# Weight tiles of two row blocks instead of one in a two-layer encoder step on one Trainium2 core

## The chip, the cores and the metric

The kernel runs on one core of one Trainium2 chip. The metric is the time of one execution on the device, in microseconds (us); a comparison takes the median of several runs. TensorE is called PE below, its weight loads PEld, VectorE DVE, ScalarE ACT, GpSimd POOL and SyncE SP, as in the profile.

## What is computed

One step of an encoder with two layers, for 384 tokens: two blocks of 128 from a prompt, and one block that holds 16 tokens of each of eight running streams. All data are 32-bit floats. Cut to what matters here:

```python
# layer 0: one projection, then two kinds of attention side by side
p  = rmsnorm(x, norm0_g) @ w_in0        # 2048 x 8200: fox q,k,v,z, stick-breaking q,k,v,z, forget logits
fo = softmax(q k^T * scale + F_q - F_k) @ v           # F: running sums of log forget gates
so = a @ v                # a: stick-breaking weights from log_sigmoid(z) and reversed running sums
h  = x + concat(fo * silu(z), so * silu(z)) @ w_out0                     # 2048 x 2048
# layer 1: spatial gating in chunks of 128 positions
u, v, z = split(rmsnorm(h, norm1_g) @ w_in1)                             # 2048 x 12288
h  = h + (u * (W_s @ layernorm(v) + b) * silu(z)) @ w_out1               # 4096 x 2048
y  = rmsnorm(h, final_g)
```

The new keys, values, forget gates and the normalised v rows are outputs too.

## The kernel before

**How a product is formed.** A weight matrix is read in blocks of 128 rows by 512 columns. TensorE multiplies in a shortened 32-bit form (`fp32r`), so each operand is split into a high and a low part, and a product is the sum of three: high by high, high by low, low by high. A block goes through four steps. SP loads it into a tile `raw` (256 KB; L72-75, L218-220, L121). ScalarE copies it, shortened, into `whi` (L84). VectorE subtracts that from `raw` into `wlo` (L86). TensorE multiplies it with each of the three token blocks (L100 high by high, L101 by the low part of the weights, L102 by the low part of the activations): 9 matmuls. Activations are split the same way by `split` (L89-91), so L90 and L91 stand for these, and for all other splits.

**The rings.** `raw` has five buffers of 128x512 (L73), `whi` and `wlo` four each (pool `wp`, L52; a buffer is 576 elements wide, L30). A buffer comes free when its last reader is done: that of `raw` after L86, those of the parts after L102.

**Columns.** `dense_nat` (L107-126) computes 512 output columns for 384 tokens: the rows in pairs of blocks, 18 matmuls a pair, into three banks of PSUM. A pair takes 4.08 us on TensorE (18 times 0.2265, its pitch in the trace). At some pairs `between` calls other work (a hook): attention heads, transposes, splits of activations. That work is put behind the split of the pair before (L116-117).

**The stages, in order of time.**

- The first columns (k of quad 0, L280-324): `first_unit` splits block 0, block 1, then pairs, in turn with the transposes and splits of the activations (L278 is the low part of these); the order on each engine is fixed by `then`.
- `values_first` (L473-498): v of quad 0 in tiles of two row blocks by 256 columns, again 128x512 a tile.
- Four quads of four heads each (L535-657): 0 and 1 with the forgetting attention, 2 and 3 with the stick-breaking one. Each projects k, q, z and v (quad 0 v ahead of q), runs the sigmoid of z by a chain on ScalarE and VectorE (L649-653), and hangs its heads as hooks on the columns of the next (L583-588). The heads (L674-768) use both engines and have their own transfers.
- The residual columns of layer 0 (`w_out0`, L840-869). Their `raw` tiles are taken from the ring and, in turn, from buffers of the heads that are idle by then (`kcache`, `vcache`; `places`, L825-837): of 13 blocks five from the ring.
- Layer 1: two ordinary columns of v; the second has four hooks `token_sums` (L911-936) on it. Then the other columns in pairs by a scheme of seven products instead of eight ("seven", L961-1033). That code has its own tiles, `sraw`, `shi` and `slo`, of 128x1024 (L941-950), loaded by 512 KB, and its own pool.
- Two ordinary columns of z and u, then the output projection `w_out1` in four rounds of `out1` (L1179-1186). Beside these the spatial gating of eight chunks is prepared (L1215-1259): its gate is transposed (L1255) and split (L1257). The last four row blocks are split early into spare buffers by `last_split` (L1319-1323).

**What sets the order.** Within the rules above a scheduler orders the instructions of each engine, with a timing model of its own that runs when the program is built; so the places of instructions move when durations or buffers change, also where the source doesn't.

## Time and profile before

| | |
|---|---|
| median of 3 runs | 1742.53 us (1740.14 to 1742.74) |
| profiled execution | 1743.44 us, span in the profile 1741.7 |
| TensorE busy | 1728.0 us, 99%, granted clock at full speed in all slices |
| VectorE, ScalarE, GpSimd busy | 1290.0 (74%), 828.2 (48%), 363.6 (21%) |
| DMA | 424.41 MB, mean 244 GB/s |
| splits of ordinary tiles | 450 on ScalarE (0.630 us each), 450 on VectorE (0.700) |
| splits of 128x1024 in the seven-product columns | 280 on each (1.061 and 1.220) |

How to read it: the span is divided between work and waits for each engine. A row of a group names the line, the engine, the operation and output <- inputs, then busy time and the mean of one, then idle time just before these instructions with what ended most of it. "PEld d L101 <- DVE wlo L86: 2.1, 7, 0.5" in the table of waits reads: weight loads for L101 waited for the VectorE instruction of L86, 2.1 us in 7 waits, the longest 0.5. A row of the timeline gives start, duration, engine, line, operation, tiles, and in brackets an idle time and what ended it. Since TensorE is busy nearly all the time, its waits are what to look for.

### The profile page before, as it was taken

How to read it: one execution, taken by the hardware profiler on the slowest of the kernel's cores; microseconds unless marked ns; L12 is line 12 of the kernel's file. 1: busy time of each engine (PE TensorE's matmuls, PEld its weight loads, DVE VectorE, ACT ScalarE, POOL GpSimd, SP SyncE). 2: the span in 40 equal slices, each digit the busy share in tenths (PEclk: the TensorE clock that was granted, in tenths of full speed). 3: DMA queues.
4: the chain of work that ended last, by engine and by line, in shares of the span. 5: the costliest groups of instructions: out<-in, count | busy, mean ns of one | idle time of the engine just before them, and what ended most of it. 6: DMA issues, size and time to landing. Idle time of an engine off the chain costs nothing. (4 is left out here: it accounts for less than half of the span.)

```text
span 1741.7 us, 23995 instructions
## 1 busy us (share of the span) xinstructions
PE 1728.0 (99%) x8323; PEld 1426.8 (82%) x8323; DVE 1290.0 (74%) x1794; ACT 828.2 (48%) x1259; POOL 363.6 (21%) x517
## 2 busy tenths in 40 slices
PE   9999999999999999999999999999999999999998
PEld 8988888887887888888878888888888887888887
DVE  6337566448347555589999999999998887787766
ACT  5435344337336344455545555555554543343344
POOL 6425544212312211100200100000000033423200
PEclk9999999999999999999999999999999999999999
DMA  8788989868877877769998989888988679879653
GB/s 233 189 226 187 279 216 223 239 184 206 235 211 186 254 195 163 188 204 333 304 304 298 313 275 320 285 294 272 320 292 271 220 248 339 255 228 305 181 159 114
DMA packets 235498, 424.41 MB, mean 244 GB/s; under 512 B 22552, under 2 KB 66128, under 8 KB 235376
## 3 DMA queue, kind: packets, MB, share of 16 engines
q1 hardware_dynamic: 174992, 312.40, 58.2%
q0 software_dynamic: 29552, 94.34, 20.0%
q10 hardware_dynamic: 30832, 16.13, 3.2%
q8 instruction: 65, 1.06, 0.3%
q14 instruction: 57, 0.47, 0.1%
HBM read 374.48 MB, written 48.29 MB: 243 GB/s over the span
## 5 line engine op out<-in xcount | busy, mean ns | idle before, releaser
L101 PE MATMUL d<-wlo,slot 128*128 128x512 f32 x1389 | 540.5, 390 | 0.2
L102 PE MATMUL d<-whi,slot 128*128 128x512 f32 x1389 | 539.8, 390 | 0.3 <-DVE slot L91 0.3
L86 DVE TENSOR_TENSOR wlo<-raw,whi 128x512 fp32r<-128x512 f32 x450 | 310.4, 700 | 306.4 <-ACT whi L84 305.1
L84 ACT ACTIVATE whi<-raw 128x512 fp32r<-128x512 f32 x450 | 281.5, 630 | 457.2 <-PE d L102 363.4
L100 PE MATMUL d<-whi,slot 128*128 128x512 f32 x1389 | 493.9, 391 | 0.8 <-ACT whi L84 0.6
L90 ACT ACTIVATE shi<-sraw 128x1024 fp32r<-128x1024 f32 x280 | 296.0, 1061 | 265.5 <-DVE sraw L970 115.5
L91 DVE TENSOR_TENSOR slo<-sraw,shi 128x1024 fp32r<-128x1024 f32 x280 | 336.6, 1220 | 25.5 <-ACT shi L90 24.1
L100 PEld LDWEIGHTS d<-whi,slot 128*128 128x128 f32 x1389 | 260.4, 188 | 59.2 <-issue 1.8
L101 PEld LDWEIGHTS d<-wlo,slot 128*128 128x128 f32 x1389 | 260.8, 188 | 55.1 <-DVE wlo L86 2.1
L102 PEld LDWEIGHTS d<-whi,slot 128*128 128x128 f32 x1389 | 260.7, 188 | 54.9 <-DVE slot L91 0.7
L958 PE MATMUL a<-slo,slot 128*128 128x512 f32 x720 | 280.5, 390 | 0.6 <-DVE slo L91 0.6
L957 PE MATMUL a<-shi,slot 128*128 128x512 f32 x720 | 264.8, 391 | 1.4 <-ACT shi L90 1.2
L970 DVE TENSOR_TENSOR sraw<-sraw,sraw 128x1024 f32<-128x1024 f32 x160 | 195.1, 1219 | 4.6 <-DMA sraw<-in_w_in_dram 4.3
L957 PEld LDWEIGHTS a<-shi,slot 128*128 128x128 f32 x720 | 135.0, 188 | 34.2 <-ACT shi L90 5.0
L958 PEld LDWEIGHTS a<-slo,slot 128*128 128x128 f32 x720 | 135.1, 188 | 29.2 <-DVE slo L91 1.5
L959 PE MATMUL a<-shi,slot 128*128 128x512 f32 x400 | 155.7, 389 | 0.0
L959 PE MATMUL a<-shi,suml 128*128 128x512 f32 x320 | 124.5, 389 | 0.0
L959 PEld LDWEIGHTS a<-shi,slot 128*128 128x128 f32 x400 | 75.1, 188 | 15.8
L1054 POOL DMA_DIRECT2D gd<-slot x7 | 3.9, 557 | 346.9 <-DVE slot L898 346.9
L464 POOL DMA_DIRECT2D slot<-d x48 | 44.1, 924 | 136.8 <-DVE wlo L86 54.2
L959 PEld LDWEIGHTS a<-shi,suml 128*128 128x128 f32 x320 | 60.1, 188 | 12.5
L957 PE MATMUL d<-shi,slot 128*128 128x512 f32 x160 | 62.3, 389 | 0.0
(311 smaller groups left out, 1840.0 us busy)
## 6 DMA issues: line engine op xcount, KB each, us to landing
sraw<-in_w_in_dram SPq DMA_DIRECT2D x320, 512.0 KB, 5.2
raw<-in_w_in_dram SPq DMA_DIRECT2D x320, 256.0 KB, 4.1
raw<-in_w_out_dram SPq DMA_DIRECT2D x175, 256.0 KB, 4.5
slot<-d POOLq DMA_DIRECT2D x48, 192.0 KB, 5.4
d<-slot ACTq DMA_DIRECT2D x24, 256.0 KB, 3.9
vd<-slot POOLq DMA_DIRECT2D x8, 768.0 KB, 4.7
gd<-slot POOLq DMA_DIRECT2D x8, 768.0 KB, 6.6
v<-vd POOLq DMA_DIRECT2D x8, 768.0 KB, 8.7
```

The costliest lines, as they stand in the source:

```text
L84: highs.append(S.activation(hi, raw, AF.Copy).ins)
L86: splits.append(V.tensor_tensor(out=lo, in0=raw, in1=f32(hi), op=ALU.subtract).ins)
L90: S.activation(hi_out, src, AF.Copy)
L91: return V.tensor_tensor(out=lo_out, in0=src, in1=f32(hi_out), op=ALU.subtract).ins
L100: PE.matmul(o, lhsT=his[k][:, t], rhs=hi[:, 0, :], start=(k == first), stop=False)
L101: PE.matmul(o, lhsT=his[k][:, t], rhs=lo[:, 0, :], start=False, stop=False)
L102: mm = PE.matmul(o, lhsT=los[k][:, t], rhs=hi[:, 0, :], start=False, stop=(k == last))
L464: r = G.dma_start(blk[32 * j:32 * j + 32].rearrange("p h (a d) -> p (h a) d", d=32), d[:, :, 32 * j:32 * j + 32].rearrange("h (a p) d -> p ...
L957: PE.matmul(o, lhsT=xh, rhs=hi[:, j, :], start=(opens and u + j == 0), stop=False)
L958: PE.matmul(o, lhsT=xh, rhs=lo[:, j, :], start=False, stop=False)
L959: PE.matmul(o, lhsT=xl, rhs=hi[:, j, :], start=False, stop=(ends and u == 3 and j == 1))
L970: return V.tensor_tensor(out=out, in0=x, in1=y, op=op)
```

## The change

All ordinary weight tiles hold two row blocks. A pair of `dense_nat` is one transfer of 512 KB, one copy on ScalarE and one subtraction on VectorE, both 128x1024; TensorE reads each half as before. `raw` has three buffers of 128x1024, `whi` and `wlo` two each, 1088 elements wide; per partition the rings take 29,696 bytes in place of 28,672. `values_first` takes four row blocks of 256 columns a tile in place of two, and its two hooks move from tiles 4 and 7 of 8 to tiles 2 and 3 of 4. In the first columns blocks 0 and 1 are still loaded and split apart, each pair of loads sharing a raw tile, while from block 2 on a pair is split at once. `places` gives whole tiles, three of seven from the ring. `last_split` loads single blocks into halves of a raw tile. The unused `eight` goes. The seven-product columns are not touched.

The instructions: 7711 on PE in both; ACT has 943 in place of 1216, DVE 1446 in place of 1706, SP 617 in place of 862. In the changed kernel the lines of this text have other numbers: L84 is L91, L86 is L93, L90/91 are L97/98, L100/101/102 are L107/108/109, L649/650 are L655/656 (and L651 L657), L731 is L737, L739 is L745, L1140 is L1132, L1184 is L1176, L1255 is L1247.

```diff
-WPITCH = 576
+WPITCH = 1088
...
-    wp = ctx.enter_context(tc.tile_pool(name="wp", bufs=4))
+    wp = ctx.enter_context(tc.tile_pool(name="wp", bufs=2))
...
-    def wload(src, nk, ncols, queue=nc.sync):
-        raw = wp.tile([P, nk, ncols], F32, tag="raw", bufs=5, name=nm("raw"))
-        queue.dma_start(raw, src.rearrange("(k p) c -> p k c", p=P))
+    def wraw(nk=2):
+        return wp.tile([P, nk, 1024 // nk], F32, tag="raw", bufs=3, name=nm("raw"))
+    def whalf(tag):
+        return wp.tile([P, WPITCH], F32R, tag=tag, name=nm(tag))
+    def wload(src, nk=2):
+        raw = wraw(nk)
+        nc.sync.dma_start(raw, src.rearrange("(k p) c -> p k c", p=P))
         return raw
-    def wunit(src, nk, ncols, raw=None, behind=()):
...
+    def halves(tag):
+        return whalf(tag)[:, :1024].rearrange("p (k c) -> p k c", k=2)
+    def wunit(raw, behind=()):
+        hi = halves("whi")
...
+        lo = halves("wlo")
         splits.append(V.tensor_tensor(out=lo, in0=raw, in1=f32(hi), op=ALU.subtract).ins)
-        return hi, lo
+        return [(hi[:, j:j + 1, :], lo[:, j:j + 1, :]) for j in range(2)]
...
-            ws = []
-            for k in (kp, kp + 1):
-                src = w[(k0 + k) * P:(k0 + k + 1) * P, c0:c0 + 512]
-                raw = raws() if raws else None
-                if raw is not None:
-                    nc.sync.dma_start(raw, src.rearrange("(k p) c -> p k c", p=P))
-                ws.append(wunit(src, 1, 512, raw, behind=behind))
+            raw = (raws and raws()) or wraw()
+            nc.sync.dma_start(raw, w[(k0 + kp) * P:(k0 + kp + 2) * P, c0:c0 + 512].rearrange("(k p) c -> p k c", p=P))
+            ws = wunit(raw, behind=behind)
...
         def load_raw():
             k = len(raws)
-            raws.append(wload(w_in0[k * P:(k + 1) * P, 1024:1536], 1, 512))
+            if k % 2 == 0:
+                both.append(wraw())
+            raws.append(both[k // 2][:, k % 2:k % 2 + 1, :])
+            nc.sync.dma_start(raws[k], w_in0[k * P:(k + 1) * P, 1024:1536].rearrange("(k p) c -> p k c", p=P))
...
-                nxt = [first_unit(k) for k in groups[i + 1]]
+                nxt = first_unit(groups[i + 1])
...
-            for u in range(KT // 2):
-                if u in (4, 7) and between:
+            for u in range(KT // 4):
+                if u > 1 and between:
...
-                raw = wload(w_in0[u * 256:(u + 1) * 256, c0:c0 + 256], 2, 256)
+                raw = wload(w_in0[u * 512:(u + 1) * 512, c0:c0 + 256], 4)
...
-                if n % 13 < 5:
+                if n % 7 < 3:
                     yield None
...
+                if not spare:
+                    both = wraw()
+                    spare.extend(both[:, j, :] for j in range(2))
+                raw = spare.pop(0)
+                nc.sync.dma_start(raw, wlast(*ck))
```

**How the order moves.** On TensorE, at the start of a pair in the q columns of quad 0, before (d are the three banks, slot_128 and slot_129 the high and low parts of the activations, whi_1198/wlo_1200 the first block, whi_1204 the second):

```order
L100 MATMUL d_1131<-whi_1198,slot_128 128x512
L100 MATMUL d_1132<-whi_1198,slot_128 128x512
L100 MATMUL d_1133<-whi_1198,slot_128 128x512
L101 MATMUL d_1131<-wlo_1200,slot_128 128x512
L102 MATMUL d_1131<-whi_1198,slot_129 128x512
L100 MATMUL d_1131<-whi_1204,slot_128 128x512
L101 MATMUL d_1132<-wlo_1200,slot_128 128x512
```

And after (one tile whi_1070/wlo_1072 for both blocks):

```order
L107 MATMUL d_1039<-whi_1070,slot_124 128x512
L107 MATMUL d_1040<-whi_1070,slot_124 128x512
L107 MATMUL d_1041<-whi_1070,slot_124 128x512
L108 MATMUL d_1039<-wlo_1072,slot_124 128x512
L109 MATMUL d_1039<-whi_1070,slot_125 128x512
L107 MATMUL d_1039<-whi_1070,slot_124 128x512
L108 MATMUL d_1039<-wlo_1072,slot_124 128x512
```

In both, three high-by-high products stand first. Before, the fourth matmul needs the low part of the first block; after, it needs that of the whole pair.

On ScalarE, where the heads of quad 2 and the sigmoid of its z run (pr, z and l are the heads' tiles, gz and slot_4192 the sigmoid's), before:

```order
L733 ACTIVATE l_4272<-l_4272 128x384
L733 ACTIVATE l_4283<-l_4283 128x288
L649 ACTIVATE slot_4192<-gz_4188 128x512 x3
L650 ACTIVATE slot_4192<-slot_4192 128x512
L84 ACTIVATE whi_4408<-raw_4406 128x512
L650 ACTIVATE slot_4192<-slot_4192 128x512 x2
```

After:

```order
L91 ACTIVATE whi_3866<-raw_3864 128x1024
L655 ACTIVATE slot_3668<-gz_3664 128x512 x3
L745 ACTIVATE pr_3739<-z_3740 128x384
L656 ACTIVATE slot_3668<-slot_3668 128x512 x3
L745 ACTIVATE pr_3739<-z_3751 128x288
L657 ACTIVATE slot_3668<-slot_3668 128x512
L737 ACTIVATE l_3777<-z_3775 128x384
L91 ACTIVATE whi_3890<-raw_3888 128x1024
```

Before, a split stands after four operations of the sigmoid; after, seven of these and three of the heads stand between one split and the next.

On VectorE in the last stage, around the transpose of a gate (gTt) and its low half (slot_13922, in the changed kernel slot_12567), before:

```order
L86 TENSOR_TENSOR wlo_13899<-raw_13895,whi_13897 128x512
L1255 STREAM_TRANSPOSE gTt_13919<-blk_13748 128x1536
L1184 TENSOR_TENSOR slot_13593<-d_13742,slot_13593 128x512
L1184 TENSOR_TENSOR slot_13593<-d_13743,slot_13593 128x512
L1184 TENSOR_TENSOR slot_13593<-d_13744,slot_13593 128x512
L91 TENSOR_TENSOR slot_13922<-gTt_13919,slot_13921 128x1536
L86 TENSOR_TENSOR wlo_13929<-raw_13925,whi_13927 128x512
```

After:

```order
L93 TENSOR_TENSOR wlo_12544<-raw_12540,whi_12542 128x1024
L1247 STREAM_TRANSPOSE gTt_12564<-blk_12309 128x1536
L1176 TENSOR_TENSOR slot_12304<-d_12370,slot_12304 128x512
L1176 TENSOR_TENSOR slot_12304<-d_12371,slot_12304 128x512
L1176 TENSOR_TENSOR slot_12304<-d_12372,slot_12304 128x512
L93 TENSOR_TENSOR wlo_12574<-raw_12570,whi_12572 128x1024
L1132 SCALAR_TENSOR_TENSOR v_12443<-v_12443,mvr,lg_12445 128x512
L98 TENSOR_TENSOR slot_12567<-gTt_12564,slot_12566 128x1536
```

The gate's low half stood ahead of the next split of weights, and now stands behind it.

## The prediction

> **What bounds the kernel now.** I read the profile's page first, then the busy time by windows, then who waits for whom on the weight loads, then the timeline at the places where TensorE waits. The page, engine totals, TensorE's clock and the four groups that split weights into high and low parts:

> ```profile
> PE 1728.0 (99%) x8323; PEld 1426.8 (82%) x8323; DVE 1290.0 (74%) x1794; ACT 828.2 (48%) x1259; POOL 363.6 (21%) x517
> ...
> PEclk9999999999999999999999999999999999999999
> ...
> L86 DVE TENSOR_TENSOR wlo<-raw,whi 128x512 fp32r<-128x512 f32 x450 | 310.4, 700 | 306.4 <-ACT whi L84 305.1
> L84 ACT ACTIVATE whi<-raw 128x512 fp32r<-128x512 f32 x450 | 281.5, 630 | 457.2 <-PE d L102 363.4
> L90 ACT ACTIVATE shi<-sraw 128x1024 fp32r<-128x1024 f32 x280 | 296.0, 1061 | 265.5 <-DVE sraw L970 115.5
> L91 DVE TENSOR_TENSOR slo<-sraw,shi 128x1024 fp32r<-128x1024 f32 x280 | 336.6, 1220 | 25.5 <-ACT shi L90 24.1
> ```

> TensorE is busy for 1728.0 of 1741.7 us at full clock. A busy PE need not be PE at its peak, so I ask whether the width of a weight tile changes its pace. The windows answer that; the third lies in the stretch of seven-product columns, which already uses tiles of 128x1024:

> ```profile
> 410.00:426.00 16.00, 15.90 (x71) 12.83 (x70) 13.80 (x30) 15.29 (x33) 3.39 (x4) 1.00 0.94 213
> 750.00:800.00 50.00, 50.00 (x223) 41.39 (x222) 47.01 (x72) 28.56 (x40) 3.00 (x5) 1.00 0.79 277
> 1250.00:1300.00 50.00, 50.00 (x222) 41.19 (x221) 47.40 (x48) 28.38 (x31) 0.53 (x1) 1.00 0.87 294
> ```

> Columns: window, its length, then busy time and count of PE, PEld, DVE, ACT, POOL, clock, DMA share. 50 us hold 221 to 222 weight loads on ordinary tiles (second row) and on wide ones (third): 0.226 us a matmul in both. The change alters neither the number of matmuls nor their pace. It can change the time only through TensorE's waits. Today these are few:

> ```profile
> PEld a L957 <- ACT shi L90: 5.0, 12, 1.3
> PEld d L101 <- DVE wlo L86: 2.1, 7, 0.5
> PEld d L100 <- ACT whi L84: 1.6, 3, 0.8
> ```

> The last two are all that TensorE waits for ordinary weight tiles: 3.7 us. That is the most that better feeding of these tiles can win. The first belongs to the seven-product columns, whose code isn't touched.

> **The cost of the splits.** Two narrow splits take 2 x 0.630 on ScalarE and 2 x 0.700 on VectorE, a wide one 1.061 and 1.220: 0.20 and 0.18 us less for each two blocks. Neither engine sets the end, so this is worth nothing by itself. What matters is how late a tile may be. A steady place of before, with the reads of the old tile, the split and the first reads of the new one:

> ```profile
> 304.90 0.19 PEld L102 LDWEIGHTS d<-whi,slot 128*128 128x128 f32 x1
> 305.58 0.19 PEld L102 LDWEIGHTS d<-whi,slot 128*128 128x128 f32 x1
> ...
> 309.88 0.64 PEld L100 LDWEIGHTS d<-whi,slot 128*128 128x128 f32 x3
> 310.56 0.19 PEld L101 LDWEIGHTS d<-wlo,slot 128*128 128x128 f32 x1
> ...
> 305.55 1.31 ACT L84 ACTIVATE whi<-raw 128x512 fp32r<-128x512 f32 x2 [4.43 <-PE d L102]
> ...
> 306.21 1.37 DVE L86 TENSOR_TENSOR wlo<-raw,whi 128x512 fp32r<-128x512 f32 x2 [1.87 <-ACT whi L84]
> ```

> The first block's buffer is read last at 304.90, ScalarE starts 0.65 later, the first low part is there at 306.21 + 0.69 = 306.90 and is read at 310.56: 3.7 us to spare. A wide buffer comes free only with its second block, read last at 305.58. So 305.58 + 0.65 = 306.23, the high part ends at 307.29, the low part at 307.29 + 0.03 + 1.22 = 308.54; the new order also reads three high parts first, so it is needed at 310.56: **2.0 us to spare**. The slack falls by 1.7 us everywhere. Where nothing else is late this costs nothing: the tile being read, 18 matmuls or 4.08 us, hides the split. Where ScalarE, VectorE or a load is more than 2.0 us late, TensorE now waits. I go through these places.

> [...]

> *Start.* Blocks 2 and 3 become one tile, in a ring where blocks 0 and 1 take a whole tile each.

> ```profile
> 8.76 1.30 ACT L282 ACTIVATE whi<-raw 128x512 fp32r<-128x512 f32 x2 [0.77 <-DMA raw<-in_w_in_dram]
> ...
> 11.49 0.39 PE L101 MATMUL d<-wlo,slot 128*128 128x512 f32 x1
> 11.72 0.40 PE L102 MATMUL d<-whi,slot 128*128 128x512 f32 x1
> ...
> 10.70 1.14 DVE L278 SCALAR_TENSOR_TENSOR slot<-a,gT,slot 128x384 fp32r<-128x384 f32 x2
> ```

> The wide split starts between 8.76 and 9.4 (its second half waits for its load), so the low part ends between 11.1 and 11.7, and the low part of the activations, 0.57 of VectorE behind it, between 11.7 and 12.3, for reads at 11.49 and 11.72. 0 to 0.6 us late; I take 0.3.

> *First quad, loads late.* Around 100 us ScalarE waits for the loads themselves:

> ```profile
> 97.38 0.63 ACT L84 ACTIVATE whi<-raw 128x512 fp32r<-128x512 f32 x1 [4.76 <-DMA raw<-in_w_in_dram]
> 100.02 0.63 ACT L84 ACTIVATE whi<-raw 128x512 fp32r<-128x512 f32 x1 [2.02 <-DMA raw<-in_w_in_dram]
> 102.50 0.63 ACT L84 ACTIVATE whi<-raw 128x512 fp32r<-128x512 f32 x1 [1.85 <-DMA raw<-in_w_in_dram]
> ...
> 101.31 0.64 PEld L100 LDWEIGHTS d<-whi,slot 128*128 128x128 f32 x3
> ...
> 103.18 0.19 PEld L100 LDWEIGHTS d<-whi,slot 128*128 128x128 f32 x1 [0.78 <-ACT whi L84]
> ```

> Today TensorE works on the block of 100.02 from 101.31 while that of 102.50 lands, and waits 0.9 in all. As one tile nothing of them can start before 102.50: high part at 103.56, 2.25 after 101.31; low part at 104.81, another 0.57 over. That is 2.8, or +1.9 on today's. Against it, three raw tiles hold six blocks where five buffers held five, so a load can be issued one block (9 matmuls, 2.0 us) earlier; if all of that arrives, the wait goes (-0.9). The middle is +0.5; I take +1.0, because the loads here are paced by their landing, about 2.5 us a block, and not by their issue.

> *Stick-breaking quads, ScalarE late.* In the window 410 to 426 above ScalarE is busy 15.29 of 16 us, and a low part is late there, and again at the next quad:

> ```profile
> 412.87 1.66 ACT L649 ACTIVATE slot<-gz 128x512 f32<-128x512 f32 x3
> ...
> 421.45 0.19 PEld L101 LDWEIGHTS d<-wlo,slot 128*128 128x128 f32 x1 [0.52 <-DVE wlo L86]
> ...
> 559.75 0.19 PEld L101 LDWEIGHTS d<-wlo,slot 128*128 128x128 f32 x1 [0.49 <-DVE wlo L86]
> ```

> The split was 3.7 + 0.5 = 4.2 late. Four pairs of splits save 0.8 of that; past the new slack of 2.0 it waits 1.4, 0.9 more than now. By the new order the longest stretch between two splits has seven operations of 128x512 (0.55 each, the first row) and three small ones (about 0.4): 5.1 + 1.06 against 4.08 is 2.1 late, at the edge of the slack, which would end today's 0.5. Between -0.5 and +0.9 each; the chain between ScalarE and VectorE that made today's wait is not in that count, so I take +0.45 each, +0.9.

> *Residual columns of the first layer.* A load lands late:

> ```profile
> 703.88 0.63 ACT L84 ACTIVATE whi<-raw 128x512 fp32r<-128x512 f32 x1 [7.04 <-DMA raw<-in_w_out_dram]
> 704.70 1.87 ACT L84 ACTIVATE whi<-raw 128x512 fp32r<-128x512 f32 x3 [0.18 <-DMA raw<-in_w_out_dram]
> ...
> 704.57 0.53 PEld L100 LDWEIGHTS d<-whi,slot 128*128 128x128 f32 x3 [0.66 <-ACT whi L84]
> ```

> Now 0.6 is lost. A wide split could start at 704.70: high part at 705.76, 1.8 after TensorE was ready at 703.95, low part 0.6 more: 2.4, or +1.8; one block earlier, -0.6. I take +0.7. *Token sums* (second window): VectorE is busy 47.01 of 50 us; the splits give back 12 x 0.18 = 2.2 us of that, the lost slack takes 1.7 from each tile: 0 to +1.0, I take +0.3.

> *Last stage.* Transposed blocks of the gate hold up both splitting engines:

> ```profile
> 1528.72 1.49 ACT L90 ACTIVATE slot<-gTt 128x1536 fp32r<-128x1536 f32 x1 [3.93 <-DVE gTt L1255]
> ...
> 1532.78 0.19 PEld L101 LDWEIGHTS d<-wlo,slot 128*128 128x128 f32 x1 [0.18 <-DVE wlo L86]
> ...
> 1672.18 0.19 PEld L101 LDWEIGHTS d<-wlo,slot 128*128 128x128 f32 x1 [0.19 <-DVE wlo L86]
> ```

> Twice the slack of 3.7 was just used up. Carried over, 3.85 late less 0.38 saved less 2.0 is a wait of 1.5, +1.3 each. But the new order puts the low half of the gate block behind the next split instead of ahead of it, which takes 1.7 us out of the way. 0 to +2.6; I take +1.3.

> SP issues half as many of these loads, each twice as large, and no wait is added to its queue; ACT's and POOL's own transfers keep their places. I cost that at nothing: a load has about 10 us from its buffer's release to its use (three tiles of 4.08 less the split).

> **The sum.** 0.3 + 1.0 + 0.9 + 0.7 + 0.3 + 1.3 = +4.5 us. The profiled execution took 1743.44 (span 1741.7), so 1747.9; the median of the runs shown is 1742.53, 0.9 below, so I forecast a median of 1747.0. The upper ends give 0.6 + 1.9 + 1.8 + 1.8 + 1.0 + 2.6 = 9.7 (1752.2), the lower ones 0 - 0.9 - 1.0 - 0.6 + 0 + 0 = -2.5 (1740.0). About 0.2%, 3.5 us, is what a measurement here can tell from no change.

> **The rivals.** *The order absorbs it.* The instructions were ordered anew with the wide tiles in view; three reads of high parts stand first and the gate's low half was moved. If that and the sixth block in flight hold wherever I took a middle, the terms cancel: 1742 to 1745. For it speaks that the steady tile keeps 2.0 us; against it, that the late loads aren't seen by any order.

> *Faster: the waits go.* If the sixth block in flight brings each late load 2.0 us forward, and the splitting engines run ahead by the 0.2 us they save a pair, all 3.7 us of waits for ordinary tiles vanish: 1742.5 - 3.7 = 1738.8. It decides at the load of 102.50: that has to land before 100.5. Against it: loads paced by landing. [...]

> ```profile
> sraw<-in_w_in_dram SPq DMA_DIRECT2D x320, 512.0 KB, 5.2
> raw<-in_w_in_dram SPq DMA_DIRECT2D x320, 256.0 KB, 4.1
> ```

> A double load lands 1.1 us later than a single one, which takes back half of the 2.0 us.

> *Heavier: late loads count double.* The high part waits for its load on 22 occasions today:

> ```profile
> ACT whi L84 <- DMA raw<-in_w_out_dram: 22.2, 14, 7.0
> ...
> ACT whi L84 <- DMA raw<-in_w_in_dram: 13.1, 8, 4.8
> ```

> From landing to low part a tile takes 2.3 us instead of 1.3. If half of them reach TensorE with that 1.0, 22 x 0.5 = 11: 1753.5. Against it: most now end with slack to spare.

> **How the numbers follow.** The forecast (waits of 3.5 to 8 us) 0.40, absorbed 0.33, faster 0.09, heavier 0.18. A tenth of the forecast's cases fall under 3.5, and some absorbed ones reach past it; so slower 0.57, same 0.34, faster 0.09. The range 1740 to 1754 takes in the sum's two ends and most of the heavier case, and leaves out the faster one and the far end of the heavier.

> **What would show it.** PE's matmul pitch stays 0.226 us. The waits of L107 and L108 on the wide splits grow from 3.7 to some 8 us, at the places named: about 100, 420, 560, 704 and in the last stage. ACT's and DVE's busy time falls by about 45 and 40 us with no gain from it. Wrong would be waits that stay at 3.7 or less, or a pitch that moves, or a wait at a place that isn't named and that alone makes more than 3 us.

## The result and the profile after

The changed kernel takes **1745.2 us** (median of 22 runs, 1741.86 to 1748.61), the kernel before 1742.03 (22 runs, 1740.14 to 1745.08). The ratio is 1.0016, 95% interval 1.0011 to 1.0022: slower by 3.2 us or a little under 0.2%. One execution among all runs, the second of the kernel with narrower buffers below, took 2915 us at a mean granted clock of 0.556 and is left out. The profiled execution took 1743.96 (span 1742.3). The page of the changed kernel, engine totals and the two groups of wide splits:

```profile
PE 1728.7 (99%) x8323; PEld 1428.6 (82%) x8323; DVE 1260.0 (72%) x1543; ACT 785.1 (45%) x1008; POOL 364.7 (21%) x517
...
L93 DVE TENSOR_TENSOR wlo<-raw,whi 128x1024 fp32r<-128x1024 f32 x226 | 279.6, 1237 | 349.1 <-ACT whi L91 349.1
...
L91 ACT ACTIVATE whi<-raw 128x1024 fp32r<-128x1024 f32 x226 | 239.3, 1059 | 526.1 <-PE d L109 435.5
```

ScalarE works 43 us less and VectorE 30, with 251 fewer instructions in the profile on each, and TensorE's time differs by 0.7. Half as many splits win nothing here: of ScalarE's 526.1 us of idle time before them 435.5 are ended by TensorE, and VectorE's 349.1 by ScalarE. The table of waits of the weight loads (line, what it waited for, us in total, times, longest):

```profile
PEld a L961 <- ACT shi L97: 5.6, 13, 1.3
PEld d L107 <- ACT slot L97: 2.2, 1, 2.2
PEld d L107 <- ACT whi L91: 1.7, 4, 0.6
...
PEld d L108 <- DVE wlo L93: 1.0, 2, 0.7
...
PEld d L108 <- DVE wlo L293: 0.6, 1, 0.6
```

The waits on wide splits come to 3.3 us here, no more than the 3.7 of before. New is the wait of 2.2 on the gate (slot, L97). A loss of 3.2 us in the median can't be read from this pair of profiles: they differ by 0.6 us of span. Single executions of both kernels vary by several us, so one profile of each is not enough, and I took both again (spans 1743.2 and 1740.0). Every profile holds 8323 matmuls, so matmul number 600, 800 and so on is nearly the same place in all. The time of each stretch between two such numbers, less its time in the second profile of before:

```
from-to us   98   140    665   756   813   1440  end    all
before       -0.3  0.7   0.3   0.3   0.0   0.4   0.2    1.8
before again  0     0     0     0     0     0     0      0
changed       0.4  0.2  -0.7   0.5   0.6  -0.3   1.5    2.3
changed again 0.1  1.2  -0.7   1.4   0.6  -0.7   1.3    3.2
```

The columns end at the time above them; they are the start, the loads at about 106 us, the quads, the residual columns at 704 us, the beginning of the seven-product columns, the rest of these, and the last stage. So the change loses at the start, at 106 and 704 us, at 789 us and in the last stage, and gains in the quads.

### The profile page after: what moved, and what is told of

Read it like the earlier page. It is cut to its first block, busy times and chain, and to the rows that moved or that the text cites. A ratio compares the mean times of both kernels' runs of the same rounds, so it can differ in the third digit from the quotient of the medians.

```text
span 1742.3 us, 22541 instructions
## 1 busy us (share of the span) xinstructions
PE 1728.7 (99%) x8323; PEld 1428.6 (82%) x8323; DVE 1260.0 (72%) x1543; ACT 785.1 (45%) x1008; POOL 364.7 (21%) x517
## 3 DMA queue, kind: packets, MB, share of 16 engines
q8 instruction: 65, 1.06, 0.3%
## 5 line engine op out<-in xcount | busy, mean ns | idle before, releaser
L108 PE MATMUL d<-wlo,slot 128*128 128x512 f32 x1389 | 542.0, 390 | 0.5 <-DVE wlo L93 0.3
L93 DVE TENSOR_TENSOR wlo<-raw,whi 128x1024 fp32r<-128x1024 f32 x226 | 279.6, 1237 | 349.1 <-ACT whi L91 349.1
L107 PE MATMUL d<-whi,slot 128*128 128x512 f32 x1389 | 493.0, 392 | 2.0 <-ACT slot L97 1.8
L91 ACT ACTIVATE whi<-raw 128x1024 fp32r<-128x1024 f32 x226 | 239.3, 1059 | 526.1 <-PE d L109 435.5
L97 ACT ACTIVATE shi<-sraw 128x1024 fp32r<-128x1024 f32 x280 | 295.9, 1061 | 263.4 <-DVE sraw L974 117.0
L98 DVE TENSOR_TENSOR slo<-sraw,shi 128x1024 fp32r<-128x1024 f32 x280 | 336.6, 1221 | 27.2 <-ACT shi L97 26.0
L107 PEld LDWEIGHTS d<-whi,slot 128*128 128x128 f32 x1389 | 260.8, 188 | 59.8 <-ACT slot L97 2.2
L108 PEld LDWEIGHTS d<-wlo,slot 128*128 128x128 f32 x1389 | 261.2, 188 | 55.6 <-DVE wlo L93 1.0
L974 DVE TENSOR_TENSOR sraw<-sraw,sraw 128x1024 f32<-128x1024 f32 x160 | 195.2, 1220 | 2.9 <-DMA sraw<-in_w_in_dram 2.6
## 6 DMA issues: line engine op xcount, KB each, us to landing
sraw<-in_w_in_dram SPq DMA_DIRECT2D x320, 512.0 KB, 5.3
raw<-in_w_in_dram SPq DMA_DIRECT2D x152, 512.0 KB, 4.3
raw<-in_w_out_dram SPq DMA_DIRECT2D x82, 512.0 KB, 4.8
d<-slot ACTq DMA_DIRECT2D x24, 256.0 KB, 5.0
```

Of the source, the lines that this page charges most:

```text
L91: highs.append(S.activation(hi, raw, AF.Copy).ins)
L93: splits.append(V.tensor_tensor(out=lo, in0=raw, in1=f32(hi), op=ALU.subtract).ins)
L97: S.activation(hi_out, src, AF.Copy)
L98: return V.tensor_tensor(out=lo_out, in0=src, in1=f32(hi_out), op=ALU.subtract).ins
L107: PE.matmul(o, lhsT=his[k][:, t], rhs=hi[:, 0, :], start=(k == first), stop=False)
L108: PE.matmul(o, lhsT=his[k][:, t], rhs=lo[:, 0, :], start=False, stop=False)
```

## The experiments

**Both kernels again.** No edit.

> The changed kernel once more, unaltered, for a second profile. The first profile holds +0.95 us at the start, +1.15 us between 1464 and 1472 us (there one unbroken wait of 1.85 us is followed by 3.5 us at about half the clock) and -1.6 us of vanished waits, +0.5 in all, while the medians differ by 3.2. Place theory: the same places carry the difference, and a slower run holds more time at a low clock. Slack theory: a slower run holds many small waits of the weight loads on the wide splits instead, all over the ordinary columns. Both: 1744 to 1747 us.

Measured 1745.01 us (11 runs), ratio 1.0019 (1.0010 to 1.0028).

> The kernel before once more, unaltered, for a second profile: its first profile (1743.44 us) lies 1.4 above the median of its runs. Place theory: the late loads at about 102 and 704 us vary in this kernel too, but between 0 and 0.7 us each, since a late narrow load costs its own lateness alone; the stretch at 1464 to 1471 us waits about 2 us in pieces of at most 1.3, with no low clock. Slack theory: many small waits of the weight loads vary, not these places. Both: 1740.5 to 1744 us.

Measured 1742.09 us (8 runs), ratio 1.0001 (0.9991 to 1.0011). Before: the place 704 us in the second profile (ScalarE, VectorE, then the weight loads that waited):

```profile
702.64 0.63 ACT L84 ACTIVATE whi<-raw 128x512 fp32r<-128x512 f32 x1 [6.54 <-DMA raw<-in_w_out_dram]
703.89 1.88 ACT L84 ACTIVATE whi<-raw 128x512 fp32r<-128x512 f32 x3 [0.62 <-DMA raw<-in_w_out_dram]
...
703.32 0.53 PEld L100 LDWEIGHTS d<-whi,slot 128*128 128x128 f32 x3 [0.16 <-ACT whi L84]
704.05 0.19 PEld L101 LDWEIGHTS d<-wlo,slot 128*128 128x128 f32 x1 [0.20 <-DVE wlo L86]
```

The changed kernel again:

```profile
703.83 1.06 ACT L91 ACTIVATE whi<-raw 128x1024 fp32r<-128x1024 f32 x1 [6.73 <-DMA raw<-in_w_out_dram]
...
704.92 1.23 DVE L93 TENSOR_TENSOR wlo<-raw,whi 128x1024 fp32r<-128x1024 f32 x1 [6.56 <-ACT whi L91]
...
704.94 0.53 PEld L107 LDWEIGHTS d<-whi,slot 128*128 128x128 f32 x3 [1.20 <-ACT whi L91]
706.20 0.19 PEld L108 LDWEIGHTS d<-wlo,slot 128*128 128x128 f32 x1 [0.73 <-DVE wlo L93]
```

Before, the first block has landed at 702.64 and TensorE begins 0.68 later, while the second lands. Wide, nothing starts before 703.83, TensorE begins 1.11 after that, and the low part makes it wait once more, 0.73. The same late load, about one step dearer on each engine. So of the two theories that of the places holds: they carry the difference, and there are no small waits everywhere.

**Splits by halves in the ordinary columns, all of them.** The buffers and loads stay wide:

```diff
-            highs.append(S.activation(hi, raw, AF.Copy).ins)
+            for j in range(2):
+                highs.append(S.activation(hi[:, j:j + 1], raw[:, j:j + 1], AF.Copy).ins)
...
+        for j in range(2):
+            splits.append(V.tensor_tensor(out=lo[:, j:j + 1], in0=raw[:, j:j + 1], ...).ins)
```

> The changed kernel with its wide buffers and loads, but in the ordinary columns each half of a tile is split by an instruction of its own (128x512), as before the change. Slack theory (the width of the split instruction costs, since the low part of the whole pair is late): back to 1742 to 1743 us. Place theory: the wait at 1465 us and the start stay, so 1744 to 1746 us; only 0.3 to 0.6 us of waits on the low part in the last stage go.

Measured 1747.64 us (7 runs), ratio 1.0029 (1.0018 to 1.0040): slower than both forecasts. In its profile the waits at 106 and 704 us are gone, but the new order of the program puts the reads of the second chunk's gate behind a wait of POOL, and TensorE stands still for 3.73 us:

```profile
1455.28 3.67 POOL L1245 DMA_DIRECT2D blk<-md  x4 [7.54 <-PE d L111]
...
1468.85 0.79 PE L109 MATMUL d<-whi,slot 128*128 128x512 f32 x1 [3.73 <-ACT slot L99]
```

In the changed kernel these reads start at 1450.15. A second wait, of 1.42 us at 1604 us, costs another 3.8 with what surrounds it, and behind both the clock falls (0.58 in the window from 1470 to 1475 us, 0.83 in that from 1600 to 1610). So this run says nothing about the width of the split in the last stage; it says what a moved order costs there.

**Wide loads alone.** The kernel before with raw tiles of two blocks and one load a pair:

```diff
-        raw = wp.tile([P, nk, ncols], F32, tag="raw", bufs=5, name=nm("raw"))
+        return wp.tile([P, nk, 1024 // nk], F32, tag="raw", bufs=3, name=nm("raw"))
...
-WPITCH = 576
+WPITCH = 528
```

> The kernel before, with the wide loads alone: raw tiles of two row blocks, three buffers, one load of 512 KB a pair; the splits stay 128x512 in four buffers each (528 elements wide instead of 576, for space). Theory that the sixth block in flight took away the wait at 102 us: that wait (0.6 us) is gone here too, and 1741.4 to 1742.4 us. Theory that wide loads arrive late and vary: 1744 to 1746 us, with waits of the high part on its load.

Measured 1765.12 us (4 runs), ratio 1.0135 (1.0121 to 1.0149). Both theories missed: the loss is spread evenly over the ordinary columns, where TensorE hardly waits but has a longer pitch, by about 0.0045 us a matmul. The exception is the last stage, where TensorE waits 4.43 us for the high part of a gate. The narrower buffer was a second edit, made for space, so I tried it by itself.

**The width of the buffers alone.** The kernel before with `WPITCH = 528`, nothing else.

> The kernel before with one constant changed: the buffers of the split parts are 528 elements wide instead of 576; the order of all engines stays. In the run with wide loads alone, which had that width too, each of the 4167 matmuls of the ordinary columns took about 0.0045 us longer. Theory that the distance of the buffers did it: the same here, 4167 x 0.0045 = 19 us, 1759 to 1763 us. Rival, the wide raw tiles did it: 1742 us.

Measured 1760.56 us, one execution. The page's rows for the matmuls of ordinary columns, with longer means than before (390 and 391 ns):

```profile
L101 PE MATMUL d<-wlo,slot 128*128 128x512 f32 x1389 | 545.9, 394 | 0.0
...
L100 PE MATMUL d<-whi,slot 128*128 128x512 f32 x1389 | 498.8, 395 | 0.2 <-ACT slot L90 0.2
```

Its span of 1758.9 is 18.9 above that of the second profile of before: the forecast 4167 x 0.0045 = 19. The order of every engine is that of before, so the width of the buffer did it here; by what way no run shows. Against this run, which has the same buffers, the wide loads, with the order that comes with them, differ by 0.5 us or less in every stretch but the last, and lose 4.6 there, at the wait named above. So these two profiles show no loss by the wide loads themselves, and none of the gain that was hoped for at 106 us either (0.2 more).

**The second gate chunk earlier.**

```diff
-        first_plan = [..., times(1, 2, 7, 8, 9, 10, 11, 12), times(2, 11, 14, 15)]
+        first_plan = [..., times(1, 2, 6, 7, 8, 9, 10, 11), times(2, 11, 14, 15)]
```

> The changed kernel with the preparation of the second gate chunk hung one pair of blocks earlier, so that its transpose and split lie ahead of the third chunk's. Place theory: the wait of 1.85 us at 1465 us goes, and with it 1.75 us of low clock behind it: 3 to 3.6 us less than the changed kernel, 1741.5 to 1742.5 us, and no stretch of low clock. Slack theory: at most the wait itself, 1743.3 to 1745 us.

Measured 1751.02 us (5 runs), ratio 1.0052 (1.0040 to 1.0065). The wait on the gate went, and a larger one came in its place:

```profile
1465.12 1.06 ACT L91 ACTIVATE whi<-raw 128x1024 fp32r<-128x1024 f32 x1 [9.96 <-DMA raw<-in_w_out_dram]
...
1466.22 1.65 PE L107 MATMUL d<-whi,slot 128*128 128x512 f32 x3 [5.36 <-ACT whi L91]
```

That load of weights took 16.7 us to land, against 10.5 at most for the loads of `raw` in the changed kernel at this time (1430 to 1470 us). The DMA engines are busy in both (a share of 1.02 to 1.10 from 1450 to 1470 us, and of 1.00 to 1.06 in the changed kernel). That the transfers brought forward delayed it is likely, but not shown. A moved step must be counted with its transfers, and as a test of the clock the run decides nothing.

**The second gate's transpose first.** Only VectorE's order changes:

```diff
+            with ExitStack() as first_gate:
+                if c == 2:
+                    first_gate.enter_context(tc.issue_after(gates[1]))
                 vh, vl = split_values(c)
```

> The changed kernel with one row moved on VectorE: the transpose of the second chunk's gate stands ahead of the third chunk's value splits (x3) instead of behind them. No transfer moves for it. Clock theory: TensorE then waits about 1.4 us at 1464 to 1467 us, but in pieces under 1.1 (each value split in turn), the clock stays full, and the 1.75 us of low clock go: 2 to 2.5 us less than the changed kernel, 1742.6 to 1743.3 us. Rival, the low clock has nothing to do with the length of one wait: it stays, and 1744.5 to 1745.3 us.

Measured 1745.72 us (11 runs), ratio 1.0015 (1.0006 to 1.0024): no gain. The clock stayed full in its profile (1.00 in every window up to 1740 us), but the wait did not break into pieces. It is 2.05 us in one, on the value split instead of the gate:

```profile
1468.63 0.49 PE L1234 MATMUL a<-vl,wTh 128*128 128x512 f32 x1 [2.05 <-DVE vl L98]
```

So the theory that one long wait lowers the clock failed in the form in which I had put it. The stretch of the wait in the changed kernel, first profile (windows of 5 us; clock, DMA share and GB/s are the last three columns):

```profile
1465.00:1470.00 5.00, 3.15 (x9) 2.28 (x8) 3.44 (x3) 1.48 (x1) 0.03 (x1) 0.74 1.04 370
1470.00:1475.00 5.00, 5.00 (x21) 4.04 (x21) 0.68 (x1) 1.06 (x1) 0.00 (x0) 0.92 1.04 346
```

And in the run with another start (below), which has the same order here and the same wait:

```profile
1468.22 0.50 PE L107 MATMUL d<-whi,slot 128*128 128x512 f32 x1 [1.85 <-ACT slot L97]
```

```profile
1465.00:1470.00 5.00, 3.04 (x14) 1.97 (x13) 4.52 (x3) 1.91 (x2) 1.14 (x2) 1.00 1.04 373
1470.00:1475.00 5.00, 4.98 (x22) 4.13 (x23) 0.78 (x1) 1.06 (x1) 0.00 (x0) 1.00 1.06 375
```

The same 1.85 us is followed by 3.41 us of low clock in one execution and by none in another: by low clock in 4 of the 7 profiles that have it (1.84 in the run with two loads a tile), and not after the 2.05. The traces show what tells them apart. In the changed kernel's first profile the clock is recorded as full from 6.49 to 1467.40 us, as half for 3.413, and as full again until 1737.05, at the end of the program. The two full stretches, of 1460.90 and 266.24 us, are 428 and 78 times 3.4133; the one of before, of 1730.56, is 507 times that. So from the start of the low stretch to the fall at the end are 79 such steps. They are 79 also in the three other profiles of the table with a low stretch: by the clock in the windows the fall at the end lies at 1738.4, 1736.8 and 1745.2, to 0.1 us. Counted back from the fall in the other four (1736.8, 1736.2, 1735.4 and about 1741.1), the ends of the steps fall inside the waits. In these eight profiles the clock is low for the step behind a wait that lies whole within one step, and stays full where the end of a step cuts the wait (us from the start of the span):

```
                          wait              parts by step   low clock from
changed                   1465.30-1467.14   1.85            1467.40
changed again             1466.35-1468.20   1.85            1468.75
layer 0, start by halves  1464.23-1466.08   1.85            1467.16
two loads a tile          1472.44-1474.28   1.84            1475.56
start by halves           1466.38-1468.22   0.83 + 1.02     none
layer 0 by halves         1464.79-1466.64   1.70 + 0.15     none
residual by halves        1465.37-1467.21   0.32 + 1.52     none
gate's transpose first    1466.58-1468.63   1.38 + 0.67     none
```

A bound in us does not follow: two low stretches, in the run with all columns by halves and in that with two loads, come after only 1.6 and 1.3 us without a matmul (waits of 0.16 and 1.42 before 1603.74; 8.70 us of TensorE's time in the window from 790 to 800, with the clock at 0.83).

**The start by halves.**

```diff
-            then("ACT", lambda: S.activation(hi, raw, AF.Copy))
+            for j in range(n):
+                then("ACT", lambda: S.activation(hi[:, j:j + 1], raw[:, j:j + 1], AF.Copy))
```

and the same for VectorE's subtraction.

> The changed kernel with the first columns' pairs split by two instructions of 128x512 on each engine; all else, and the order of TensorE, is the same. Place theory: the start loses the 0.6 to 0.95 us that it gained over before: 1744.2 to 1744.5 us. Rival, the start is late through the shared raw tile and the two loads, not through the wide split: no change, 1745 us.

Measured 1744.3 us (11 runs), ratio 1.0011 (1.0002 to 1.0019), 0.7 below the changed kernel. In its profile the start takes 0.3 us less than in the second profile of before, against 0.1 to 0.4 more in the changed kernel. The medians alone would not tell it. The stretch does: less its time in the second profile of before, the start takes +0.1 to +0.8 us in the eight profiles with wide splits there and buffers of 1088 elements. In the four with splits of 128x512 there and buffers of 576 or 1088 elements it takes -0.6 to 0. What it undoes, in the changed kernel (first profile):

```profile
9.61 1.06 ACT L289 ACTIVATE whi<-raw 128x1024 fp32r<-128x1024 f32 x1 [1.45 <-DMA raw<-in_w_in_dram]
10.70 1.23 DVE L293 TENSOR_TENSOR wlo<-raw,whi 128x1024 fp32r<-128x1024 f32 x1 [1.76 <-ACT whi L289]
11.98 0.19 PEld L108 LDWEIGHTS d<-wlo,slot 128*128 128x128 f32 x1 [0.60 <-DVE wlo L293]
```

**Layer 0 by halves, and parts of it.** As in the second experiment, but the splits are whole again from layer 1 on, whose order is that of the changed kernel on every engine:

```diff
+    apart = [slice(0, 1), slice(1, 2)]
...
+            for js in apart:
+                highs.append(S.activation(hi[:, js], raw[:, js], AF.Copy).ins)
...
         calc_rstd(ssq1)
+        apart[:] = [slice(0, 2)]
```

> The changed kernel with the ordinary columns of layer 0 alone split by halves (two instructions of 128x512 on each engine, the buffers and loads still wide); layer 1 has the same order on all engines. Place theory: a load that lands late at 106 or 704 us costs 0.9 us less (0.45 of the high part and 0.45 of the low part), so the two places cost 1 to 1.8 us less, and the quads stay free of waits: 1743.3 to 1744.1 us. Rival, the width of the instruction doesn't matter there and the lateness of the 512 KB load does: 1745 us, with the waits at 106 and 704 us as large as in the changed kernel.

Measured **1742.1 us** (11 runs), ratio 0.9998 (0.9990 to 1.0007): all that the change lost is back, more than forecast. The step behind a late load can be compared at 106 us, first in the changed kernel again (ScalarE, then the weight loads), then in this run:

```profile
105.31 1.06 ACT L91 ACTIVATE whi<-raw 128x1024 fp32r<-128x1024 f32 x1 [6.25 <-DMA raw<-in_w_in_dram]
...
106.42 0.53 PEld L107 LDWEIGHTS d<-whi,slot 128*128 128x128 f32 x3 [0.72 <-ACT whi L91]
...
107.67 0.19 PEld L108 LDWEIGHTS d<-wlo,slot 128*128 128x128 f32 x1 [0.73 <-DVE wlo L93]
```

```profile
106.45 1.15 ACT L94 ACTIVATE whi<-raw 128x512 fp32r<-128x512 f32 x2 [7.21 <-DMA raw<-in_w_in_dram]
...
107.13 0.53 PEld L111 LDWEIGHTS d<-whi,slot 128*128 128x128 f32 x3 [1.35 <-ACT whi L94]
107.86 0.19 PEld L112 LDWEIGHTS d<-wlo,slot 128*128 128x128 f32 x1 [0.20 <-DVE wlo L97]
```

TensorE starts 1.11 us behind the landing with the wide split and 0.68 with halves, and the low part is waited for 0.73 and 0.20: 0.96 less in all, near the forecast 0.9. In sum the stretch shows no gain in this profile (1.3 us above before again): the load lands at 106.45, later than in any other profile with wide tiles. With the wide split and a landing at 106.15, in the run with the gate first, the stretch costs 1.9. With the start by halves as well:

> The changed kernel with both edits of the two runs before: the pairs of the first columns and the ordinary columns of layer 0 are split by halves, layer 1 keeps wide splits. Place theory: the gains add, 0.7 us less than with layer 0 alone: 1741.2 to 1741.6 us, 0.5 to 1 us below the kernel before. Rival, the 3 us that layer 0 gave held a share of the start or were chance: 1742 us or more.

Measured 1742.52 us (11 runs), ratio 0.9998 (0.9988 to 1.0007). The gains do not add in the medians. The start did lose its time (0.6 us less than before), but this profile has the low clock at 1465 us, 1.1 us. With halves in the residual columns alone:

> The changed kernel with halves in the residual columns of layer 0 alone (the stretch around 704 us); everything before and after has wide splits as in the changed kernel. Counted from the profiles, the stretch cost 0.5 to 1.7 us in the changed kernels and -0.1 to 0.4 in the two with all of layer 0 by halves. Place theory: 0.7 to 1.2 us less than the changed kernel, 1743.8 to 1744.3 us, and the wait of the low part there is gone. Rival, the 3 us that layer 0 by halves gave came from the earlier columns (or elsewhere): 1745 us.

Measured 1743.29 us (11 runs), ratio 1.0009 (1.0000 to 1.0018), 1.7 below the changed kernel. The stretch at 704 us takes 0.2 us less than in before again, and no weight load waits there. But the halves are not all that differs. SP's queue in this run and in the changed kernel again, first the one with halves, then the other:

```profile
681.59 9.17 SPq L130 DMA_DIRECT2D raw<-in_w_out_dram  x3
690.81 0.46 SPq L168 DMA_DIRECT2D slot<-in_x_prompt_dram  x1
691.32 0.46 SPq L169 DMA_DIRECT2D slot<-in_x_sample_dram  x1
693.88 4.40 SPq L130 DMA_DIRECT2D raw<-in_w_out_dram  x2
```

```profile
682.07 5.07 SPq L126 DMA_DIRECT2D raw<-in_w_out_dram  x2
688.66 0.37 SPq L164 DMA_DIRECT2D slot<-in_x_prompt_dram  x1
689.08 0.46 SPq L165 DMA_DIRECT2D slot<-in_x_sample_dram  x1
690.28 8.48 SPq L126 DMA_DIRECT2D raw<-in_w_out_dram  x3
```

With halves the scheduler puts one more load of weights ahead of the two loads of x (768 KB). In the changed kernel that load stands behind them, is issued at 690.28 and split at 703.83: the loads of that time take up to 13.4 us to land, as a view of that tile below shows. So the late load is one of place in the queue, and a wide split makes it dearer (by 0.96 us at 106). The time from issue to landing of the loads into `raw` in the changed kernel again, 684 to 707 us:

```profile
DMA to landing us min/median/max: 4.1/8.1/13.4
```

How much each of the two gives back at 704 us, these runs do not separate.

**Two loads a tile.** The changed kernel with each tile filled by two loads of 256 KB:

```diff
-            nc.sync.dma_start(raw, w[(k0 + kp) * P:(k0 + kp + 2) * P, c0:c0 + 512].rearrange("(k p) c -> p k c", p=P))
+            for j in range(2):
+                nc.sync.dma_start(raw[:, j], w[(k0 + kp + j) * P:(k0 + kp + j + 1) * P, c0:c0 + 512])
```

> The changed kernel with each wide raw tile of the ordinary columns filled by two loads of 256 KB instead of one of 512 KB; buffers and splits stay wide. Place theory (the width of the split makes a late load dear): the split waits for both loads anyway, so 1744.4 to 1745.6 us, with a high and a low wait at 106 and 704 us as in the changed kernel. Rival, the load of 512 KB lands late by its size: 1742.5 to 1743.8 us, with those waits gone or halved.

Measured 1750.72 us (6 runs), ratio 1.0042 (1.0027 to 1.0057). The late load stays, and so does the low part's wait behind it:

```profile
705.87 0.53 PEld L107 LDWEIGHTS d<-whi,slot 128*128 128x128 f32 x3 [2.08 <-ACT whi L91]
707.12 0.19 PEld L108 LDWEIGHTS d<-wlo,slot 128*128 128x128 f32 x1 [0.73 <-DVE wlo L93]
```

The size of the load isn't what makes it late. By its stretches this kernel loses 3.9 us at 704 us and 3.8 just behind, both followed by low clock (0.88 in the window from 700 to 710 us, 0.83 from 790 to 800); the cause of the second was not tried.

## Why the prediction was right, and where not

The forecast was 1747.0 us, +4.5; measured are 1745.2 and +3.2. That is slower beyond its interval, and inside the bound of 0.2% that the prediction set for telling it from no change: it lies where the forecast case begins and the case of the order that absorbs it (1742 to 1745) ends. The terms against the stretches: the mean of the two profiles of before is subtracted from the mean of the profiles that are like the changed kernel in that stretch (the changed kernel twice, and the runs with the second chunk earlier, the gate first and the start by halves, each left out where its edit is; from 756 us on also the three runs with halves in layer 0 or a part of it, whose order behind 722 us is that of the changed kernel on every engine).

```
                         predicted   measured
start                      +0.3       +0.4    (4 profiles)
first quad, loads at 106   +1.0       +0.8    (5)
stick-breaking quads       +0.9       -0.7    (5)
residual columns, 704      +0.7       +0.9    (5)
token sums                 +0.3       +0.6    (8)
seven-product columns       0         -0.4    (8)
last stage                 +1.3       +0.4    (6: +1.4, +1.2, +1.0, -0.2, -0.3, -0.4)
sum                        +4.5       +2.1    (before rounding)
```

The medians differ by 3.2, 1.1 more than this sum, a difference that single profiles varying by 1 us leave open; the two profiled executions of the changed kernel lie 1.2 and 0.1 us below the medians of their runs. That the forecast comes within 1.8 us of the median is in part luck: the quads came out 1.6 us below their term and the last stage 0.9, and the low clock, which the prediction has nowhere, makes up for part of it.

- **Pace.** Right. The window of 50 us of the changed kernel (TensorE, its weight loads, VectorE, ScalarE, GpSimd) holds 219 weight loads in 49.71 us of TensorE's time, 0.227 each (the busy time that the two splitting engines save, 43 and 30 us against about 45 and 40, is worth nothing, as forecast):

```profile
750.00:800.00 50.00, 49.71 (x220) 40.84 (x219) 46.13 (x63) 27.13 (x31) 2.49 (x5) 1.00 0.78 279
```

- **Start.** Right in place and size; undone, it comes back.
- **Late loads.** Right in mechanism. The prediction worked the low part's extra wait out as 0.57 at the load of 102.50 us; there, now at 106 us, and at 704 the weight loads wait 0.73 for it after each late high part (changed kernel again). The sixth block in flight did not bring the loads forward: in the ten profiles with wide tiles and buffers of 1088 elements the load at 106 us lands between 103.67 and 106.45, and its stretch costs 0 to 1.9 us more than in the second profile of before. SP's queue, which the prediction costed at nothing with about 10 us from a buffer's release to its use, is part of the wait at 704: there a load takes 13.4 us to land.
- **Stick-breaking quads.** Wrong, in sign. The prediction says "the chain between ScalarE and VectorE that made today's wait is not in that count, so I take +0.45 each". The count of operations had given -0.5 each, and it came nearer. The changed kernel's ScalarE at the place:

```profile
412.75 1.06 ACT L91 ACTIVATE whi<-raw 128x1024 fp32r<-128x1024 f32 x1 [0.41 <-PE d L109]
...
418.52 1.04 ACT L91 ACTIVATE whi<-raw 128x1024 fp32r<-128x1024 f32 x1
```

  From the end of one split to the next the ten operations take 4.7 us (counted 5.1), and TensorE does not wait; the waits of before on the low part are gone: at 420 us in nine of the ten profiles with wide tiles (the run with the second chunk earlier waits 0.39), at 559 in eight. At 420 us it is gone with halves too, so the width of the split is not what took it away. That the new order did is likely, but no run moves the order alone there. With this term at -0.7 and the rest as forecast the sum is +2.9.
- **Token sums.** Within its bounds, but the wait is one place behind: the first seven-product tile waits for its high part at 789 us, where the stretch loses 0.6 in each of the eight profiles. Before has no wait there. The run with all ordinary columns by halves has it too, so the width of the split does not make it; what does was not tried.
- **Last stage.** Wrong in mechanism, and in size but for the low clock. The low parts were to wait 1.3 us each at about 1532 and 1672. In the changed kernel none does: at 1531 us the weight loads wait 0.55 for a high part, at 1537 us 0.44 for a transposed block (wTh), and at 1672 for nothing. What counts is one place, where the transposed second gate holds TensorE for 1.85 us. Before, the waits there came to 1.58 in three pieces (before again, TensorE):

```profile
1465.56 0.39 PE L1239 MATMUL a<-vl,wTh 128*128 128x256 f32 x1 [1.07 <-DVE vl L91]
...
1466.50 0.50 PE L100 MATMUL d<-whi,slot 128*128 128x512 f32 x1 [0.21 <-ACT slot L90]
...
1468.43 0.50 PE L102 MATMUL d<-whi,slot 128*128 128x512 f32 x1 [0.30 <-DVE slot L91]
```

  In the six profiles with this order the last stage loses 1.0 to 1.4 us where the low clock follows, and gains 0.2 to 0.4 where it does not. TensorE in the changed kernel after the wait:

```profile
1467.14 0.60 PE L107 MATMUL d<-whi,slot 128*128 128x512 f32 x1 [1.85 <-ACT slot L97]
1467.54 0.63 PE L108 MATMUL d<-wlo,slot 128*128 128x512 f32 x1
1467.97 0.63 PE L107 MATMUL d<-whi,slot 128*128 128x512 f32 x1
```

On the low clock: in the eight profiles of the table above its changes lie on steps of 3.413 us, and the same wait of 1.85 us had a low clock behind it in 4 profiles of 7, by its place between the steps. The matmuls behind it start 0.43 apart in place of 0.2265 (1467.54 and 1467.97 above); eight of them cost 1.6 us.

**The rivals.** That the waits vanish was refuted at its own condition, the load that was to land before 100.5 us. Nor does a double load land 1.1 us later than a single one: loads of `w_in` into `raw` take 4.3 us in the median with 512 KB (changed kernel) and 4.1 with 256 KB (before). That the late loads count double was too dear, as few of the 22 reach TensorE (waits of L107 on the high part: 4 of 1.7 us and 5 of 3.2 in the two profiles). A loss was absorbed in the quads alone.

What stays open: layer 0 by halves gave 3.0 us in the median. By its one profile, about 1.2 of that comes from 704 us, where the moved load has its share, and the rest from places that vary from run to run (the low clock, the seven-product columns), or from the place at 106 us, where a late load costs 0.96 less but landed late in that profile. The share of the low clock in the medians is open too. Of 33 executions of the changed kernel six have a mean granted clock of 0.997 (median 1746.95 us) and eleven one of 0.999 (1743.56). Of 90 of the kernel before one has 0.997 and 48 have 0.999. A stretch of 3.41 us at half the clock takes 0.001 off the mean. No version was measurably faster than before.

## What to carry to other kernels

Making tiles wider on engines that are not the bound won nothing here, and it cost where a load was late: nothing starts before all of the tile is there, and each engine's step of the chain is longer (1.06 us in place of 0.63 on ScalarE, 1.23 in place of 0.70 on VectorE). So look for the two or three latest loads, keep the steps there narrow, and see where in the queue they stand. One wait of TensorE of 1.85 us cost another 1.6 by the low clock behind it, in four profiles of seven. Where a scheduler orders the program, an edit also moves rows elsewhere, and one profile of each kernel is not enough to tell 3 us: compare stretches between the same instructions over several profiles.
